# A decoder layer's attention projections: PSUM banks emptied by ScalarE copies, one ring of buffers, attention's loads queued later, last branch in another order

## The chip, the cores and the metric

The kernel runs on one core of one Trainium2 chip. A core has TensorE (PE: matmuls from SBUF into eight PSUM banks), VectorE (DVE), ScalarE (ACT), GpSimd (POOL) and SyncE (SP, whose queue issues most of the DMA loads here); each engine works through its own list of instructions in order. The metric is the device time of one execution in microseconds, and the time of a kernel is the median of its runs.

## The reference

A layer with 1024 tokens, width 1024, in fp32. One projection of h = RMSNorm(x) gives all inputs of three branches: A (attention of each query over 256 keys, which a small indexer picks), B (latent attention) and M (attention over 256 memory tokens). Each branch has a SiLU gate path z and a sigmoid merge gate.

```python
proj = h @ w_in[layer]
q_a = partial_rope(rms_norm(q_a.reshape(b, s, A_HEADS, A_HEAD_DIM), g_qn_a[layer]), cos_a, sin_a)
k_a = partial_rope(rms_norm(k_a.reshape(b, s, A_HEADS, A_HEAD_DIM), g_kn_a[layer]), cos_a, sin_a)
o_a = dsa_attention(q_a, k_a, v_a, q_i, k_i, w_i)
...
ys = jnp.stack([o_a * jax.nn.silu(z_a), o_b * jax.nn.silu(z_b), o_m * jax.nn.silu(z_m)])
branch = jnp.einsum('nbsw,nwd->nbsd', ys, w_branch[layer])
merged = jnp.einsum('bsnd,nbsd->bsd', gates, branch)
x = x + merged @ w_out[layer]
```

RMSNorm of q and k is over the 64 elements of a head; the rotation (`partial_rope`) turns its first 16. It is linear, so a factor per token and head may be applied before it or behind it.

## The kernel before

Every fp32 product is made of three matmuls (`mm3`, L273 to L275): each operand is split into a rounded part h and a rest l, and h·h, h·l and l·h are added in PSUM. Weights are loaded by SP (L258), then ACT casts the part h (L241) and DVE subtracts it to get l (L244); an output of 512 columns over 512 channels takes 12 matmuls.

The order of the program after the latent branch and the indexer is: branch 2 (M), branch 1 (B), the last projections, attention A with the matmuls of gate 0 as filler (`f`), the last branch 0 (A), and the output projection. `branch(n)` makes the gate path z (L1269, L1270), multiplies it with the loaded attention output `osb` (L1300, L1302) and splits the result into `yh` and `yl` (L1305, L1306); this is done for four pieces w of 128 channels, each in two halves j. Then `br` matmuls go over eight output blocks d, two halves j each; the merge gate `tg` (L1318) is loaded, and `emit` multiplies it with the bank (L1340 for `ab`, L1346 for `am`) and stores into `s_acc` by a DMA that POOL issues. In branch 0 (L1551 to L1563) `ac` is loaded back, POOL adds, ACT casts `hTh` and DVE subtracts to `hTl`, which feed the output projection. Before, branch 0 takes first the pieces whose z isn't made yet (w=3), then 0, 1, 2.

`qkv(p)` (p from 0 to 3) projects q, k and v of two heads of branch A: eight token tiles of 128 tokens, each 24 matmuls of 384 columns into one PSUM bank, in two halves of four tiles. qkv(0) stands in branch 2 between the y pieces and the `br` matmuls, qkv(1) in branch 1 likewise, then come z of branch 0 for w=0 (`early(0, 1)`), qkv(2), z for w=1, qkv(3), z for w=2. Four instructions of DVE and two of ACT read a tile's bank; the last is the subtraction of the rest of v:

```python
nc.scalar.activation(sq.rearrange("p h d -> p (h d)"), ps[:, 0:256], AF.Square)
nc.vector.tensor_reduce(out=ss[:, i, :], in_=sq, op=ALU.add, axis=AX.X)
for e, dst in enumerate((xq, xk)):
    nc.vector.tensor_tensor(dst[:, i], psv[:, e], g_am[:, e:e + 1, :].to_broadcast([P, 2, 64]), op=ALU.mult)
nc.scalar.copy(vst[:, i, 0::3, :], pv)
i_ = nc.vector.tensor_tensor(vst[:, i, 1:3, :], pv, f(vst[:, i, 0::3, :]), op=ALU.subtract)
run_topk(i_, 4.2)
```

`run_topk` lets the indexer's search for the 256th largest score run in the background. Its tests are `kdj` on DVE (L1039) and `kag` on ACT (L1045), which wait for the small updates `kac`, `kar`, `kaT` on DVE; an instruction of it stands behind the given one if both are on the same engine. Per half, POOL makes the reciprocal root `rr` (L234), scales q (L1389), DVE rotates (L422 to L427) and scales k (L1392), and ACT and DVE split q (L1393, L1394). `load_k` and `load_q` (L1407, L1413) load what attention A needs first (`akd`, `aqs`); the filler's weights are `f_0_0r` and so on (L389).

Of the kernel before, what the change touches and what calls it, by code (L numbers as in the profile page):

```python
# [16 lines left out]
ALU = mybir.AluOpType  # L17
# [78 lines left out]
def f(ap):  # L96
    return ap.bitcast(F32)
# [3 lines left out]
def hybrid_kernel(  # L101
# [144 lines left out]
    def wload(pool, nm, srcs, a, n, kind=None):  # L246


        def tile(dt, tag, bufs, nm, width):
            if width is None:  # L250
                return pool.tile([P, a, n], dt, tag=tag, name=nm, bufs=bufs)
            t = pool.tile([P, width], dt, tag=tag, name=nm, bufs=bufs)
            return t[:, 0:a * n].rearrange("p (a n) -> p a n", a=a)
        width = pool_raw[2] if len(pool_raw) > 2 else None
        raw = tile(F32, "raw", pool_raw[0], nm + "r", width)
        o = 0
        for ap, w in srcs:
            nc.sync.dma_start(raw[:, :, o:o + w], ap)  # L258
# [895 lines left out]
    wkind = [None]  # L1154
# [129 lines left out]
    def branch(n, zc, wpool, wk, yp, o_T, emit, bg=None, tgb=2, wkt=None, zb=2, ob=2, mid=None):  # L1284
# [3 lines left out]
        def b_weights(d):  # L1288
            return wload(wpool, f"b{n}w{d}", [(wview(w_branch[n], 0, 4, d * P, P), P)], 4, P, wkind[0])

        for w in sorted(range(4), key=lambda w: (n, w) in z_done):
            szs = z_part(n, w, zc, wpool, wk, zb)
            if n == 0 and b0 is None:
                b0 = b_weights(0)
            h_ = yp.tile([P, S], FR, tag=f"yh{w}", name=f"yh{n}_{w}")
            l_ = yp.tile([P, S], FR, tag=f"yl{w}", name=f"yl{n}_{w}")
            for j in range(2):
                cs = slice(j * 512, (j + 1) * 512)
                osb = wk.tile([P, 512], F32, tag="osb", name=f"osb{n}_{w}_{j}", bufs=ob)
                nc.sync.dma_start(osb, o_T[w * P:(w + 1) * P, cs])  # L1300
                sz = szs(j)
                i_ = nc.vector.tensor_tensor(sz, osb, sz, op=ALU.mult)  # L1302
                if bg is not None:
                    bg(i_, 5.1)
                nc.scalar.copy(h_[:, cs], sz)  # L1305
                nc.vector.tensor_tensor(l_[:, cs], sz, f(h_[:, cs]), op=ALU.subtract)  # L1306
            yh[w], yl[w] = h_, l_
        if mid is not None:
            mid()
        for d in range(NK):  # L1310
# [3 lines left out]
            for j in range(2):  # L1314
                cs = slice(j * 512, (j + 1) * 512)
                tg = (wkt or wk).tile([P, 512], F32, tag="tg", name=f"tg{n}_{d}_{j}", bufs=tgb)
# [12 lines left out]
    with w3s as ph:  # L1329
# [20 lines left out]
        def qkv(p):  # L1350
# [7 lines left out]
            ws[:] = WSG  # L1358
            for j in range(2):
# [4 lines left out]
                ss = wk.tile([P, 4, 4], F32, tag="ass", name=nm + "ss")  # L1364
                rr = wk.tile([P, 4, 4], F32, tag="arr", name=nm + "rr")
                vst = wk.tile([P, 4, 4, 64], FR, tag="vst", name=nm + "v", bufs=1)
                qs = wk.tile([P, 4, 2, 2, 64], FR, tag="qs", name=nm + "qs", bufs=1)
                for i in range(4):
# [6 lines left out]
                    psv = ps[:, 0:256].rearrange("p (e h d) -> p e h d", e=2, h=2)  # L1375
                    sq = wk.tile([P, 4, 64], F32, tag="asq", name=f"asq{p}_{tb}", bufs=1)
                    nc.scalar.activation(sq.rearrange("p h d -> p (h d)"), ps[:, 0:256], AF.Square)
                    nc.vector.tensor_reduce(out=ss[:, i, :], in_=sq, op=ALU.add, axis=AX.X)
                    for e, dst in enumerate((xq, xk)):
                        nc.vector.tensor_tensor(dst[:, i], psv[:, e], g_am[:, e:e + 1, :].to_broadcast([P, 2, 64]),  # L1380
                                                op=ALU.mult)
# [15 lines left out]
                nc.gpsimd.dma_start(s_qa[p][j], f(qs).rearrange("p t h e d -> p (t h e d)"))  # L1397

# [23 lines left out]
        branch(2, C_ZM, wpool, wk, yp, s_om, emit_b, run_topk, tgb=3, ob=2, mid=lambda: qkv(0))  # L1422
        branch(1, C_ZB, wpool, wk, yp, s_o[1], emit_m, run_topk, tgb=3, ob=2, mid=lambda: qkv(1))
# [13 lines left out]
    wkind[0] = None  # L1437


    with ExitStack() as ph:  # L1440
# [88 lines left out]
        attention(load_gen, k_prep, q_prep, scores, pv, pool_filler(fp, take_jobs("F", NFA), FWA, FBB), PFA, PREA, GENA, LDA)  # L1529
# [5 lines left out]
    with ExitStack() as ph:  # L1535
# [7 lines left out]
        with ExitStack() as ph2:  # L1543
# [5 lines left out]
            def emit_a(d, j, tg, pb):  # L1549
# [6 lines left out]
                late.append((d, j, ac))  # L1556

# [11 lines left out]
            pre = []  # L1569

            def pre_wo(after, pe):
                pre.append(0)
                if len(pre) == PRW:
                    pool_raw[:] = [1, 8]
                    wo_load(wpa, 0)
                    pool_raw[:] = list(PRF)
# [49 lines left out]
```

## Time and profile before

| | us |
|---|---|
| median of three runs | 1425.96 (1423.29 to 1428.38) |
| profiled execution | 1430.6, its span 1428.8 |
| PE busy | 1370.9 (96%) |
| PE's weight loads | 1173.3 |
| DVE busy | 954.4 (67%) |
| ACT busy | 681.4 (48%) |
| POOL busy | 209.3 (15%) |
| granted clock of TensorE, mean | 0.987 of 2.4 GHz |

The profiled execution is the one whose trace is read below; it took 4.6 us more than the median. Times in the trace count from the span's start. The stretch of the change runs from about 710 (qkv(0)) to 1060 (attention A begins), and the last branch from about 1264 to 1330.

### The profile page before, as it was taken

Reading aid. Unit: us, or ns where it says so; the run is one execution under the profiler, and the core shown is the slowest. Engines: PE = TensorE matmul, PEld = TensorE weight load, DVE = VectorE, ACT = ScalarE, POOL = GpSimd, SP = SyncE. Lnnn points to the kernel's source line nnn. Section 1 sums busy time; section 2 is a strip of 40 time slices with the busy share of each in tenths; the row PEclk is TensorE's granted clock in tenths of the full one; section 3 lists DMA queues with packets and bytes.
Section 4 is the critical chain, followed back from the end, with each engine's and each line's share of the span. In section 5 each row is a group of like instructions: output and inputs, shape, how many; then the busy total and the mean of one; then the engine's idle time right before and its main releaser. Section 6 shows DMA issues by size and latency. Waiting matters only on the chain.

```text
span 1428.8 us, 20870 instructions
## 1 busy us (share of the span) xinstructions
PE 1370.9 (96%) x7440; PEld 1173.3 (82%) x7440; DVE 954.4 (67%) x2434; ACT 681.4 (48%) x1464; POOL 209.3 (15%) x240
## 2 busy tenths in 40 slices
PE   7999999999999999999999999997999999988998
PEld 5998888888888889877897898796978888866787
DVE  5935446678888851578868777667868888756411
ACT  6635533356666652455655564433245666543200
POOL 3150004511102000000013004204220000004200
PEclk9999999999999999999999999998999999999999
DMA  7411222321111131012416532973151442175532
GB/s 246 135 45 54 77 58 86 114 56 41 49 56 53 45 104 46 23 52 67 132 52 231 164 85 89 255 165 118 46 180 49 126 133 59 54 234 186 185 105 71
DMA packets 154712, 147.45 MB, mean 103 GB/s; under 512 B 38000, under 2 KB 114800, under 8 KB 154608
## 3 DMA queue, kind: packets, MB, share of 16 engines
q1 hardware_dynamic: 147024, 123.58, 29.0%
q0 software_dynamic: 7008, 20.45, 4.8%
q10 hardware_dynamic: 576, 2.10, 0.4%
q8 instruction: 58, 0.95, 0.3%
q14 instruction: 46, 0.38, 0.1%
HBM read 99.43 MB, written 46.66 MB: 102 GB/s over the span
## 4 chain that ended last, share of the span: by engine, by line
PE 64%; DVE 13%; ACT 6%; issue 6%; DMA 5%; POOL 3%; SPq 0%; ACTq 0%; DVEq 0%; POOLq 0%
PE f L273 6%; PE f L274 5%; PE f L275 5%; DVE kdj L1039 2%; PE o L274 2%; PE o L273 2%; PE o L275 2%; PE br L275 2%; PE br L273 2%; ACT kag L1045 2%; PE br L274 2%; DVE idx L1233 1%; PE ixps L274 1%; PE ixps L275 1%; PE ixps L273 1%
## 5 line engine op out<-in xcount | busy, mean ns | idle before, releaser
L1045 ACT ACTIVATE kag<-idx,kaT 128x896 bf16<-128x896 f32 (+2 forms) x96 | 82.8, 862 | 42.2 <-DVE kaT L1066 37.9
L1039 DVE TENSOR_SCALAR_CACHE_REDUCE kdj<-idx,kdT 128x1024 bf16<-128x1024 f32 (+2 forms) x96 | 92.3, 962 | 0.7
L273 PE MATMUL f<-hTh,f_0h 128*128 128x512 f32 x184 | 79.4, 432 | 4.9 <-DVE sz L1270 2.8
L273 PE MATMUL f<-hTh,f_1h 128*128 128x512 f32 x184 | 76.3, 415 | 0.0
L274 PE MATMUL f<-hTl,f_0h 128*128 128x512 f32 x184 | 75.0, 408 | 0.0
L275 PE MATMUL f<-hTh,f_0l 128*128 128x512 f32 x184 | 74.9, 407 | 0.0
L275 PE MATMUL f<-hTh,f_1l 128*128 128x512 f32 x184 | 74.3, 404 | 0.0
L274 PE MATMUL f<-hTl,f_1h 128*128 128x512 f32 x184 | 73.9, 401 | 0.0
L1554 POOL TENSOR_TENSOR ac<-ac,tg 128x512 f32<-128x512 f32 x16 | 25.0, 1565 | 265.2 <-DVE tg L1552 257.3
L1596 DVE TENSOR_TENSOR xr<-o,xr 128x512 f32<-128x512 f32 x16 | 11.0, 690 | 61.8 <-PE o L275 61.8
L365 ACT ACTIVATE fo<-f 128x512 f32<-128x512 f32 x48 | 28.8, 600 | 39.9 <-PE f L275 36.0
L1227 ACT ACTIVATE irl<-is 128x512 f32<-128x512 f32 (+1 forms) x80 | 37.8, 527 | 15.6 <-DVE idx L1233 12.0
L273 PEld LDWEIGHTS f<-hTh,f_0h 128*128 128x128 f32 x184 | 35.5, 193 | 11.6 <-ACT fo L365 3.1
L1233 DVE SCALAR_TENSOR_TENSOR idx<-irl,wi,idx 128x1024 f32<-128x1024 f32 (+5 forms) x42 | 40.2, 958 | 2.5 <-ACT irl L1227 0.8
L275 PEld LDWEIGHTS f<-hTh,f_0l 128*128 128x128 f32 x184 | 35.7, 194 | 6.8
L275 PEld LDWEIGHTS f<-hTh,f_1l 128*128 128x128 f32 x184 | 34.7, 189 | 6.0
L274 PEld LDWEIGHTS f<-hTl,f_0h 128*128 128x128 f32 x184 | 35.7, 194 | 3.9
L274 PEld LDWEIGHTS f<-hTl,f_1h 128*128 128x128 f32 x184 | 34.9, 190 | 4.4
L273 PEld LDWEIGHTS f<-hTh,f_1h 128*128 128x128 f32 x184 | 35.0, 190 | 4.2
L1225 PE MATMUL is<-kih,iqT 128*128 128x512 f32 (+1 forms) x80 | 30.1, 381 | 2.7 <-ACT irl L1227 2.3
L1270 DVE SCALAR_TENSOR_TENSOR sz<-sz,z 128x512 f32<-128x512 f32 x24 | 16.3, 683 | 23.4 <-ACT sz L1269 23.4
L1174 DVE TENSOR_SCALAR wi<-ixps 128x8 f32<-128x8 f32 x8 | 1.3, 166 | 42.0 <-ACT xi L1172 42.0
(1237 smaller groups left out, 4765.4 us busy)
## 6 DMA issues: line engine op xcount, KB each, us to landing
s_tg<-fo SPq DMA_DIRECT2D x48, 256.0 KB, 2.1
tg<-s_tg SPq DMA_DIRECT2D x48, 256.0 KB, 4.7
f_0r<-in_w_in_dram SPq DMA_DIRECT2D x23, 256.0 KB, 3.2
f_1r<-in_w_in_dram SPq DMA_DIRECT2D x23, 256.0 KB, 3.2
xx<-in_x_dram SPq DMA_DIRECT2D x8, 512.0 KB, 7.2
osb<-s_o SPq DMA_DIRECT2D x16, 256.0 KB, 3.0
s_acc<-ab POOLq DMA_DIRECT2D x16, 256.0 KB, 5.1
s_acc<-am POOLq DMA_DIRECT2D x16, 256.0 KB, 6.2
```

The source lines that it names most:

```text
L273: nc.tensor.matmul(ps, ah, bh, start=start, stop=False)
L274: nc.tensor.matmul(ps, ah, bl, start=False, stop=False)
L275: nc.tensor.matmul(ps, al, bh, start=False, stop=stop)
L365: nc.scalar.activation(o, ps, AF.Tanh, scale=0.5)
L1039: nc.vector.tensor_scalar(out=junk, in0=idx[t], scalar1=T[:, i:i + 1], scalar2=0.0, op0=ALU.is_ge, op1=ALU.add, accum_out=cnt[:, i:i + 1])
L1045: nc.scalar.activation(junk, idx[t], AF.Sign, bias=T[:, i:i + 1], accum_out=cnt[:, i:i + 1])
L1225: nc.tensor.matmul(sp[:, 0:w], q_, kih[:, k0:k0 + w], start=True, stop=False)
L1227: nc.scalar.activation(rl[:, k0:k0 + m], sp[:, 0:m], AF.Relu)
L1233: i_ = nc.vector.scalar_tensor_tensor(out=acc[:, 0:n], in0=rl[:, 0:n], scalar=wc, in1=acc[:, 0:n], op0=ALU.mult, op1=ALU.add)
L1270: zi[0] = nc.vector.scalar_tensor_tensor(out=sz, in0=sz, scalar=1.0, in1=pz[j], op0=ALU.add, op1=ALU.mult)
L1554: nc.gpsimd.tensor_tensor(ac, ac, tg, op=ALU.add)
L1596: nc.vector.tensor_tensor(xr, ps, xr, op=ALU.add)
```

## The change

- In `qkv`, ACT copies q, k and v of a token tile out of the bank (three copies of 128x128), and nothing else reads the bank. Squares, sums, the gain and the split of v are then made once per half, over 512 columns.
- q and k are rotated before they are scaled by `rr`; POOL scales both (before, q on POOL and k on DVE).
- `run_topk` is given the copy of v, an ACT instruction.
- `tg`, `ab`, `am`, the copies of q, k, v and the squares share a ring of nine buffers (`t2k`); before, `tg` had three, `ab` and `am` three, the others their own.
- `load_k(0)`, `load_q(0, ·)` and the filler's first weights are put behind the last weight load of qkv(3) in SP's queue.
- Branch 0 makes z of w=3 first and then the y pieces in the order 0, 1, 2, 3; its weights `b0w` have a ring of their own, with two raw buffers instead of one; the output weights `wo` are started at the fourth output instead of the eighth y piece.

```diff
-PRF = (1, 5)
+WOD = (1, 1)
+PRF = (2, 2)
...
-        for w in sorted(range(4), key=lambda w: (n, w) in z_done):
-            szs = z_part(n, w, zc, wpool, wk, zb)
-            if n == 0 and b0 is None:
-                b0 = b_weights(0)
+        early_z = {}
+        if n == 0:
+            for w in range(4):
+                if (n, w) not in z_done:
+                    early_z[w] = z_part(n, w, zc, wpool, wk, zb)
+            b0 = b_weights(0)
+        for w in range(4):
+            szs = early_z.pop(w, None) or z_part(n, w, zc, wpool, wk, zb)
...
+        def t2k(nm):
+            return wk.tile([P, 512], F32, tag="t2k", name=nm, bufs=9)
...
         def emit_b(d, j, tg, pb):
-            ac = wk.tile([P, 512], F32, tag="ac", name=f"ab{d}_{j}", bufs=3)
+            ac = t2k(f"ab{d}_{j}")
...
-                xq = wk.tile([P, 4, 2, 64], F32, tag="xq", name=nm + "xq")
-                xk = wk.tile([P, 4, 2, 64], F32, tag="xk", name=nm + "xk", bufs=1)
+                sh = "p (t h d) -> p t h d"
+                xq, xk, xv = (t2k(f"{nm}x{c}").rearrange(sh, t=4, h=2) for c in "qkv")
...
+                    psv = ps.rearrange("p (e h d) -> p e h d", e=3, h=2)
+                    for e, x_ in enumerate((xq, xk, xv)):
+                        i_ = nc.scalar.copy(x_[:, i], psv[:, e])
                     run_topk(i_, 4.2)
+                for e, x_ in enumerate((xk, xq)):
+                    sq = t2k(f"{nm}sq{e}").rearrange("p (t d) -> p t d", t=8)
+                    nc.scalar.activation(sq, x_.rearrange("p t h d -> p (t h) d"), AF.Square)
+                    nc.vector.tensor_reduce(out=ss[:, e, :], in_=sq, op=ALU.add, axis=AX.X)
+                    nc.vector.tensor_tensor(x_.rearrange("p t h d -> p (t h) d"), x_.rearrange("p t h d -> p (t h) d"),
+                                            g_am[:, 1 - e:2 - e, :].to_broadcast([P, 8, 64]), op=ALU.mult)
                 rsqrt_mean(rr, ss, 1.0 / 64)
...
+                for e, x_ in enumerate((xk, xq)):
+                    rope(x_[:, :, :, 0:16], cos_a[:, b, :], sin_a[:, b, :], 2, 8, wk, f"ar{p}_{j}_{e}")
+                    r_ = rr[:, e, :].rearrange("p (t h) -> p t h", t=4).unsqueeze(3).to_broadcast([P, 4, 2, 64])
+                    nc.gpsimd.tensor_tensor(x_, x_, r_, op=ALU.mult)
+                nc.scalar.copy(vst[:, :, 0::3, :], xv)
+                nc.vector.tensor_tensor(vst[:, :, 1:3, :], xv, f(vst[:, :, 0::3, :]), op=ALU.subtract)
...
-        load_k(0)
-        load_q(0, 0)
-        load_q(0, 1)
         early(1, 2)
-        qkv(3)
+        a3 = qkv(3)
+        with tc.issue_after(a3.ins):
+            load_k(0)
+            load_q(0, 0)
+            load_q(0, 1)
...
+                if (d, j) == WOD:
+                    pool_raw[:] = [1, 8]
+                    wo_load(wpa, 0)
+                    pool_raw[:] = list(PRF)
```

ACT's list at the start of qkv(2), where `z0w` are the next gate path's weights, `f_0_0h` the filler's, `asq` and `a_0v` the readers of the banks `a_0` to `a_2`; before:

```order
L241 CAST z0w_0h<-z0w_0r 128x512
L241 CAST z0w_4h<-z0w_4r 128x512
L1377 ACTIVATE asq_0_10253<-a_0_10228 128x256
L241 CAST f_0_0h<-f_0_0r 128x512
L1383 CAST a_0v<-a_0_10228 128x2x64
L1377 ACTIVATE asq_1_10289<-a_1_10264 128x256
L1383 CAST a_0v<-a_1_10264 128x2x64
L241 CAST f_0_1h<-f_0_1r 128x512
L1377 ACTIVATE asq_2_10325<-a_2_10300 128x256
L1383 CAST a_0v<-a_2_10300 128x2x64
L241 CAST f_1_0h<-f_1_0r 128x512
```

and now:

```order
L241 CAST z0w_4h<-z0w_4r 128x512
L1270 ACTIVATE sz_0_1_10156<-z_0_1_10125 128x512
L1386 COPY a_0xq<-a_0_10209 128x128
L1386 COPY a_0xk<-a_0_10209 128x128
L1386 COPY a_0xv<-a_0_10209 128x128
L1386 COPY a_0xq<-a_1_10241 128x128
L1386 COPY a_0xk<-a_1_10241 128x128
L1386 COPY a_0xv<-a_1_10241 128x128
L1386 COPY a_0xq<-a_2_10273 128x128
```

The three casts of filler weights no longer stand between the readers of the banks (they are now in qkv(3)).

SP's queue at the same place, where `akd` and `aqs` are attention's first loads, `z0w` the weights of z for w=1, and `a3w0r` to `a3w3r` those of qkv(3); before:

```order
L258 DMA a2w3r<-in_w_in_dram 128x2x128 x3
L1407 DMA akd_10617<-s_ka_0_112 128x8x64
L1407 DMA akd_10617<-s_ka_1_113 128x8x64 x2
...
L1413 DMA aqs_1_10625<-s_qa_1_105 128x4x128
L258 DMA z0w_0r<-in_w_in_dram 128x4x128
L258 DMA z0w_4r<-in_w_in_dram 128x4x128
L389 DMA f_0_0r<-in_w_in_dram 128x4x128
L258 DMA a3w0r<-in_w_in_dram 128x2x128 x3
L258 DMA a3w1r<-in_w_in_dram 128x2x128 x3
L389 DMA f_0_1r<-in_w_in_dram 128x4x128
L389 DMA f_1_0r<-in_w_in_dram 128x4x128
```

and now:

```order
L258 DMA a2w3r<-in_w_in_dram 128x2x128 x2
L258 DMA z0w_0r<-in_w_in_dram 128x4x128
L258 DMA z0w_4r<-in_w_in_dram 128x4x128
L258 DMA a3w0r<-in_w_in_dram 128x2x128 x3
L258 DMA a3w1r<-in_w_in_dram 128x2x128 x3
L258 DMA a3w2r<-in_w_in_dram 128x2x128 x3
L258 DMA a3w3r<-in_w_in_dram 128x2x128 x3
L1418 DMA akd_11050<-s_ka_0_112 128x8x64 x2
...
L1424 DMA aqs_1_11058<-s_qa_1_105 128x4x128
L258 DMA z0w_0r<-in_w_in_dram 128x4x128
L258 DMA z0w_4r<-in_w_in_dram 128x4x128
L390 DMA f_0_0r<-in_w_in_dram 128x4x128
```

All weights of qkv(3) now stand ahead of attention's loads and of the filler's.

SP's queue at the start of the last branch, where `osb` and `sz` (the stored z of w=0 to 2) feed the y pieces, and `b0w2r` and `wo_0r` are weights; before:

```order
L366 DMA s_tg_99<-fo_7_1_13918 128x512
L1300 DMA osb_3_0_14007<-s_o_95 128x512
...
L1300 DMA osb_0_1_14032<-s_o_95 128x512
L258 DMA wo_0r<-in_w_out_dram 128x2x512
L1318 DMA tg_1_0_14142<-s_tg_99 128x512
L1551 DMA ac_0_14157<-s_acc 128x512
L1300 DMA osb_1_0_14041<-s_o_95 128x512
L1318 DMA tg_1_1_14163<-s_tg_99 128x512
L1254 DMA sz_0_0_14027<-s_z 128x512
...
L1300 DMA osb_1_1_14048<-s_o_95 128x512
L258 DMA wo_1r<-in_w_out_dram 128x2x512
...
L258 DMA b0w2r<-in_w_branch_dram 128x4x128
```

and now:

```order
L258 DMA b0w2r<-in_w_branch_dram 128x4x128
L258 DMA b0w3r<-in_w_branch_dram 128x4x128
...
L367 DMA s_tg_99<-fo_7_1_13878 128x512
...
L1305 DMA osb_0_0_13967<-s_o_95 128x512
L1255 DMA sz_0_0_13969<-s_z 128x512
L1305 DMA osb_0_1_13974<-s_o_95 128x512
L1255 DMA sz_0_1_13976<-s_z 128x512
L1305 DMA osb_1_0_13983<-s_o_95 128x512
L1255 DMA sz_1_0_13985<-s_z 128x512
...
L1305 DMA osb_3_1_14023<-s_o_95 128x512
...
L258 DMA wo_0r<-in_w_out_dram 128x2x512
L258 DMA b0w4r<-in_w_branch_dram 128x4x128
```

`sz_0_0` follows right behind `osb_0_0`, `b0w2r` and `b0w3r` are ahead of every load of a y piece, and `wo_0r` is behind them all.

## Rows read from the trace of the kernel before

**Rows 1.** The page, busy time: us (share of the span) xinstructions.

```profile
PE 1370.9 (96%) x7440; PEld 1173.3 (82%) x7440; DVE 954.4 (67%) x2434; ACT 681.4 (48%) x1464; POOL 209.3 (15%) x240
```

**Rows 2.** What PE waited for, 740 to 1060 us: total, times, longest.

```profile
PE a L273 <- DVE a_0v L1384: 7.0, 2, 5.8
PE a L274 <- DVE a3w3l L244: 3.8, 1, 3.8
PE br L273 <- DVE a_1v L1384: 3.3, 2, 2.4
PE f L273 <- DVE sz L1270: 2.8, 1, 2.8
PE br L273 <- DVE ab L1340: 2.3, 2, 1.4
```

**Rows 3.** The same view, 1260 to 1335 us.

```profile
PE br L275 <- DVE b0w2l L244: 4.4, 1, 4.4
PE br L273 <- ACT yh L1305: 3.9, 1, 3.9
```

**Rows 4.** Sum over the six windows at half clock: us, busy of each engine.

```profile
sum 34.50, PE 28.00 PEld 23.05 DVE 23.44 ACT 10.42 POOL 15.07; mean PE 4.67 PEld 3.84 DVE 3.91 ACT 1.74 POOL 2.51
```

**Rows 5.** One window in branch 2: us, busy (x), clock, DMA share, GB/s.

```profile
775.00:800.00 25.00, 25.00 (x108) 20.10 (x107) 19.13 (x51) 14.79 (x30) 5.39 (x10) 1.00 0.84 276
```

**Rows 6.** What ACT waited for, 935 to 975 us.

```profile
ACT z0w_0h L241 <- DMA z0w_0r<-in_w_in_dram: 5.0, 1, 5.0
...
ACT f_0h L241 <- DMA f_0r<-in_w_in_dram: 3.1, 1, 3.1
```

**Rows 7.** Timeline of SP's queue, 936 to 988 us: start, us, instruction.

```profile
936.58 4.38 SPq L1413 DMA_DIRECT2D aqs<-s_qa  x4
941.06 0.61 SPq L258 DMA_DIRECT2D z0w_0r<-in_w_in_dram  x1
...
985.24 1.39 SPq L258 DMA_DIRECT2D a3w3r<-in_w_in_dram  x3
```

**Rows 8.** ACT's groups by form, 710 to 1045 us: busy, mean ns, idle before.

```profile
L1045 ACT ACTIVATE kag<-idx,kaT 128x896 bf16<-128x896 f32 x27 | 28.1, 1043 | 38.3 <-DVE kaT L1066 36.3 <-DVE kdT L1066 2.0
...
L1377 ACT ACTIVATE asq<-a 128x256 f32<-128x256 f32 x32 | 12.1, 377 | 0.0
...
L1383 ACT CAST a_0v<-a 128x128 fp32r<-128x128 f32 x16 | 4.2, 261 | 29.3 <-DVE a_0xk L1380 29.3
L1393 ACT CAST a_0qs<-a_0xq 128x512 fp32r<-128x512 f32 x4 | 2.5, 621 | 17.7 <-DVE a_0xq L427 11.3 <-issue 6.4
```

**Rows 9.** DVE's groups by form, the same stretch.

```profile
L1392 DVE TENSOR_TENSOR a_0xk<-a_0xk,a_0rr 128x512 f32<-128x512 f32 x4 | 2.7, 683 | 0.0
```

**Rows 10.** Timeline of POOL, 1034 to 1041 us.

```profile
1035.10 2.92 POOL L234 TENSOR_TENSOR a_1rr<-a_1rr,mhalf 128x16 f32<-128x16 f32 x1
...
1038.39 1.05 POOL L1389 TENSOR_TENSOR a_1xq<-a_1xq,a_1rr 128x512 f32<-128x512 f32 x1
```

**Rows 11.** Tile `am`: its store by DMA, us to landing.

```profile
DMA to landing us min/median/max: 4.8/6.2/7.5
```

**Rows 12.** Tile `tg`, 740 to 930 us: its load, us to landing.

```profile
DMA to landing us min/median/max: 2.6/5.6/8.8
```

**Rows 13.** Timeline of SP's queue, 1264 to 1282 us.

```profile
1265.19 1.89 SPq L1300 DMA_DIRECT2D osb<-s_o  x4
...
1273.55 1.38 SPq L1254 DMA_DIRECT2D sz<-s_z  x3
...
1281.90 0.43 SPq L258 DMA_DIRECT2D b0w2r<-in_w_branch_dram  x1
```

**Rows 14.** Tile `osb`, 1264 to 1290 us: its load, us to landing.

```profile
DMA to landing us min/median/max: 2.8/4.7/5.8
```

**Rows 15.** Timeline, POOL and DVE, 1292.9 to 1296 us.

```profile
1293.74 1.10 DVE L1563 SCALAR_TENSOR_TENSOR hTl<-ac,hTh 128x512 fp32r<-128x512 f32 x1 [1.25 <-ACT hTh L1555]
```

**Rows 16.** Timeline of DVE, 1041 to 1044 us.

```profile
1042.31 1.28 DVE L1270 SCALAR_TENSOR_TENSOR sz<-sz,z 128x512 f32<-128x512 f32 x2
```

More of the change, by code (lines that the diff above doesn't have):

```diff
@@ L1315, in branch @@
                 cs = slice(j * 512, (j + 1) * 512)
[L1316 removed]
+                tg = (wkt or wk).tile([P, 512], F32, tag=tgt, name=f"tg{n}_{d}_{j}", bufs=tgb)
                 if (n, d) in gates_done:
@@ L1344, in emit_m @@
         def emit_m(d, j, tg, pb):
-            ac = wk.tile([P, 512], F32, tag="ac", name=f"am{d}_{j}", bufs=3)
+            ac = t2k(f"am{d}_{j}")
             i_ = nc.vector.scalar_tensor_tensor(out=ac, in0=tg, scalar=1.0, in1=pb, op0=ALU.add, op1=ALU.mult)
@@ L1358, in qkv @@
             ws[:] = WSG
+            last = last_load[0]
             for j in range(2):
@@ L1374, in qkv @@
                         mm3(ps, ah, al, wh[:, kt % 2, :], wl[:, kt % 2, :], kt == 0, kt == NK - 1)
[L1375 to L1381, printed above, removed]
@@ L1386, in qkv @@
                 rsqrt_mean(rr, ss, 1.0 / 64)
-                nc.gpsimd.tensor_scalar(out=rr[:, :, 0:2], in0=rr[:, :, 0:2], scalar1=64 ** -0.5,
+                nc.gpsimd.tensor_scalar(out=rr[:, 1, :], in0=rr[:, 1, :], scalar1=64 ** -0.5,
                                         scalar2=0.0, op0=ALU.mult, op1=ALU.add)
-                nc.gpsimd.tensor_tensor(xq, xq, rr[:, :, 0:2].unsqueeze(3).to_broadcast([P, 4, 2, 64]), op=ALU.mult)
-                for e, v in enumerate((xk, xq)):
-                    rope(v[:, :, :, 0:16], cos_a[:, b, :], sin_a[:, b, :], 2, 8, wk, f"ar{p}_{j}_{e}")
@@ L1397, in qkv @@
                 nc.gpsimd.dma_start(s_qa[p][j], f(qs).rearrange("p t h e d -> p (t h e d)"))
+            return last
         hds = ExitStack()
@@ L1420, in early @@
                 z_early(0, w, C_ZA, wpool, wk, run_topk)
-        branch(2, C_ZM, wpool, wk, yp, s_om, emit_b, run_topk, tgb=3, ob=2, mid=lambda: qkv(0))
-        branch(1, C_ZB, wpool, wk, yp, s_o[1], emit_m, run_topk, tgb=3, ob=2, mid=lambda: qkv(1))
+        branch(2, C_ZM, wpool, wk, yp, s_om, emit_b, run_topk, ob=2, mid=lambda: qkv(0))
+        branch(1, C_ZB, wpool, wk, yp, s_o[1], emit_m, run_topk, ob=2, mid=lambda: qkv(1))
         early(0, 1)
@@ L1528, in hybrid_kernel @@
         ws[:] = WSQ
-        attention(load_gen, k_prep, q_prep, scores, pv, pool_filler(fp, take_jobs("F", NFA), FWA, FBB), PFA, PREA, GENA, LDA)
+        fill_a = pool_filler(fp, take_jobs("F", NFA), FWA, FBB)
+        with tc.issue_after(a3.ins):
+            fill_a.run(1)
+        attention(load_gen, k_prep, q_prep, scores, pv, fill_a, PFA, PREA, GENA, LDA)
     hds.close()
@@ L1568, in hybrid_kernel @@
             pool_raw[:] = PRF
[L1569 to L1576, printed above, removed]
+            wkind[1] = ("wb", 6, 512)
             ws[:] = WSF
-            branch(0, C_ZA, wpool, wkz, yp, s_o[0], emit_a, pre_wo, 4, wk, ZB5, OB5)
+            branch(0, C_ZA, wpool, wkz, yp, s_o[0], emit_a, None, 4, wk, ZB5, OB5, tgt="tg")
             ws[:] = WSO
```

22 lines of the change are left out of this document (9 added, 13 removed).

## The prediction

> **What bounds the kernel now.** The page's first part comes first: PE is busy for 1370.9 of 1428.8 us [rows 1], so what can be won without fewer matmuls is its idle time, and time in which it works at the lower clock. Next I read what PE waited for, over the two stretches that the change touches. Between 740 and 1060 us PE waits 7.0 us for `a_0v` and 3.3 for `a_1v`, which are DVE's last reads of a projection's bank; 3.8 for the low part of qkv(3)'s last weights; 2.8 for `sz`, which holds the filler's bank; and 2.3 for `ab` [rows 2]. In the last branch it waits 4.4 us for `b0w2l` and 3.9 for the first `yh` [rows 3]. Together that is 27.5 us.
>
> Third, I looked for windows in which the granted clock is half (0.51, the level of 1.2 GHz). There are six after 800 us, at 882, 967, 994, 1042, 1278 and 1298, and each lies at one of the waits of 2.4 us or more; behind waits of 1.4 us or less there was none. In these 34.5 us PE is busy for 28.0 [rows 4], work that takes 14.0 at the full clock (2.4 GHz): they cost 14.0 us, 2.3 each on average. The ceiling for this change is so 27.5 + 14.0 = 41.5 us. The step of a matmul of 512 columns at full clock is 25.00 us / 108 = 0.23 [rows 5], an output of the branches (12 of them) 2.8.
>
> Why are the banks late? Around the longest wait (it ends at 970) ACT had stood for 5.0 us before the weights `z0w_0r` and 3.1 before `f_0r` [rows 6], and SP issued `z0w_0r` only at 941.06, behind 4.38 us of `aqs` issues [rows 7]. ACT's casts of v also stood 29.3 us for DVE's `a_0xk` [rows 8]. So ACT and DVE pass each other's delays on, and the bank comes free when both are through. In the last branch the loads of `sz` start at 1273.55, 8.4 us after the first `osb` at 1265.19, and `b0w2r` at 1281.90 [rows 13].
>
> **The change, part by part.**
>
> *Banks.* ACT's three copies per tile take at most 0.26 us each by the cast of the same shape, 0.8 against 0.38 + 0.26 before; per half ACT gets two squares and the cast of v, about 0.62 each by the cast of 512 columns [rows 8]. That is 4 × 0.14 + 3 × 0.62 = 2.4 us more per half of some 17, on an engine that is busy for 48% [rows 1]. No copy waits for DVE now, and the casts of filler weights have left this place. What is late next is ACT itself behind `kag` tests (1.04 us the longest, and 38.3 us of idle time before them [rows 8]). Bound: 10.3 us gained if ACT is always in time, nothing if the tests hold it as DVE did. Banks are reused two to four tiles later, so I take 9.3.
>
> *Weights of qkv(3).* Their last load was issued at 985.24 [rows 7]; now it is ahead of attention's and the filler's loads. Gain 3.8, bound 0 to 3.8. Attention's loads cost nothing: they have qkv(3) as cover, 192 matmuls of three quarters of 0.23, or 33 us; without it each 4.7 us (the landing of `osb`, the same 256 KB [rows 14]) would show.
>
> *The filler's bank.* `sz` was read at 1042.31 [rows 16], behind the split of q, which waited for POOL's root and product, 2.92 and 1.05 us [rows 10]. Now its first half stands ahead of that split, behind reductions, gains and rotations that need no root. The squares, sums, gains, 12 rotations and the split of v add up to about 7 us after the last tile, so some 1.5 us of the wait stays: gain 1.3, bound -1 to 2.8.
>
> *`ab`.* The wait of 1.4 came from DVE behind POOL, and goes; the other 0.9 followed a late weight, and stays. Gain 1.4.
>
> *Last branch.* `sz_0_0` follows the first `osb`, so it lands near 1265.7 + 4.7 = 1270.4 [rows 13, 14], and the first `yh` comes 1.3 us later, ahead of the end of z (about 1275.6: before, `sz` landed near 1278.2, `yh` came at 1279.5, and PE had waited for 3.9). DVE's chain of 18 operations of 0.68 [rows 9] ends near 1282.8; PE needs the last piece after some 30 matmuls, at 1282.5. `b0w2` is loaded before the branch. `b0w3l` stands behind the product of `tg_2_0` on DVE, at about 1290.9, and PE needs it at 1292.3. Both waits go, 8.3 us, but two places are just in time: gain 7.3, bound 4 to 8.3.
>
> *Clock.* If no wait of 2.4 us or more stays, all 14.0 come back; if two stay, 9.4.
>
> *The ring.* `tg` was loaded ahead of the projections; now a load waits for a buffer five outputs back. One pass is a store (6.2 [rows 11]), a load (5.6 [rows 12]) and a DVE operation (0.68): 12.5 us, and PE gives 5 × 2.8 = 13.9. With the longest landings it is 7.5 + 8.8 + 0.7 = 17.0, 3.1 too long; three passes in a branch make 9.3, less the 5.6 that PE may run ahead over its banks, plus a half clock of 2.3: 6 per branch, 12 for two. The typical landing gives nothing; as the first loads come late too, I take 4. What is queued behind such a load on SP are the next weights of the same branch.
>
> The Trainium skill, DMA: Bandwidth & Descriptors, section "Anatomy of one DMA — SWDGE (gpsimd) path", gives a DMA as about 2.0 us plus its bytes over 436 GB/s. An estimate from it for 256 KB is 2.6, so that a pass would be 5.9 us, the ring would never wait, and the sum would be 37 instead of 33. The trace doesn't agree: its median store takes 6.2 us [rows 11].
>
> *Sum.* 9.3 + 3.8 + 1.3 + 1.4 + 7.3 + 14.0 - 4 = 33 us. The profiled execution took 1430.6, so it would take about 1397.5; the median of the runs is 4.6 below it, 1425.96, and becomes 1393.
>
> **The rivals.**
>
> *The ring binds.* Landings near the long end of both rows, because copies, stores and loads now run together (the DMA share is 0.84 there already [rows 5]). The gain of 37 loses 12, and up to 7 more if weights behind a waiting load are late too: 18 to 25 us gained, 1401 to 1408. For it speaks the load of 8.8; against it the medians.
>
> *ACT is the new keeper of the banks.* If `kag` tests, each waiting for DVE's update, hold the copies for longer than the spare banks last, the 9.3 and the half clocks at three waits (7) don't come: 33 - 16 = 17 gained, 1409. For it speak 38.3 us of idle time before `kag`; against it, that qkv(2) and qkv(3), where the longest waits are, have few tests.
>
> *POOL slows DVE.* DVE's `hTl` took 1.10 us beside a POOL addition [rows 15], where operations of that shape take 0.68 [rows 9]. POOL gets eight more products of 1.05 us [rows 10]. If one meets the chain ahead of `sz`, the wait of 1.5 grows by 0.4 to 1.05, to about 2.4, and the half clock comes back: 1 + 2.3 less, 30 gained, 1396. The Trainium skill, GPSIMD Engine Reference, section "Key points", says that POOL shares its SBUF interfaces with VectorE and collides with its instructions of two SBUF inputs; by that rule this is the case, and the row agrees.
>
> *Slower than before.* One mechanism can do it: the ring's pass grows until it sets the pace of both branches. Each branch loses 3 × (L - 13.9) - 5.6. For the 37 us to be lost in two branches, L has to be 21.9 us; the longest store and the longest load together give 17.0. A store that waits behind POOL's other work, and a load behind a weight on SP, could add some us; 22 in every pass is hard to see.
>
> **How the numbers follow.** Chances: the sum as worked out, with or without POOL's part, 0.62 (own range 1385 to 1401); the ring 0.16; ACT 0.12; slower 0.05; no measurable change 0.03, if several of these meet; better than 1385, 0.02. The predicted time is 1393. The range takes in the bounds of the ring and of ACT: 1383 to 1411. About 0.3% (4 us) is what a measurement of this kernel can tell from no change: faster by more 0.92, within it 0.03, slower 0.05.
>
> **What would show it.** In the changed profile PE's waits for `a` and `br` on a DVE read of the bank are gone and those on ACT's copies are short; a3w3l is gone from the list; the windows at half clock in the last branch are gone; `b0w3l` and `yl` wait under 1 us. The prediction is wrong if PE waits in `br` for `ab` or `am` several times per branch, each after a `tg` load that waited for an `s_acc` store, if `z` or `a` waits for weights queued behind them, or if attention's first transposes wait for `akd`.

## The result, and the profile after

| | us, median (range, runs) | ratio to the kernel before, 95% interval |
|---|---|---|
| before | 1426.15 (1423.29 to 1428.38, 4) | |
| changed | 1437.66 (1436.91 to 1442.87, 4) | 1.009 [1.006, 1.0119] |

The change makes the kernel 0.9% slower, where 2.3% faster was forecast. The profiled execution took 1442.87 us, 5.2 above the median; its span is 1441.1.

The page's busy times, as in [rows 1]:

```profile
PE 1366.4 (95%) x7440; PEld 1169.4 (81%) x7440; DVE 956.4 (66%) x2338; ACT 692.7 (48%) x1520; POOL 222.8 (15%) x248
```

PE's busy time fell by 4.5 us, but its idle time grew from 57.9 to 74.7. What PE waited for between 740 and 1075 us (total, times, longest), which answers to [rows 2]:

```profile
PE br L274 <- DVE am L1354: 12.4, 5, 4.7
PE br L274 <- DVE ab L1348: 8.5, 4, 4.0
PE z L274 <- ACT kag L1046: 4.3, 1, 4.3
PE z L276 <- DVE z1w_4l L244: 2.9, 3, 1.3
PE z L274 <- ACT a_1xv L1386: 1.4, 1, 1.4
PE f L274 <- DVE sz L1271: 1.2, 1, 1.2
PE a L274 <- ACT a_0xv L1386: 1.0, 1, 1.0
```

The waits at which the change was aimed are gone or short: `a_0v` and `a_1v` have become 2.4 us on ACT's copies (before 10.3), `a3w3l` is no longer there, `sz` fell from 2.8 to 1.2. In their place stand 20.9 us for `am` and `ab`, the products with `tg`, of which 2.3 were there before. The row of `kag` most likely belongs to them: its wait ends at 948.36, just behind the branch's last `am` (947.52 to 948.21), and before, the same matmul of z waited 0.6 us for `am`; by the profile `kag` only ended a little later. The same view in the last branch, 1268 to 1350 us, answers to [rows 3]:

```profile
PE br L274 <- ACT b0w6h L241: 8.6, 1, 8.6
PE br L276 <- DVE b0w6l L244: 1.6, 1, 1.6
PE br L274 <- ACT yh L1310: 1.2, 1, 1.2
PE br L276 <- DVE b0w3l L244: 0.6, 1, 0.6
```

Here too the old waits went (`yh` and `b0w2l`, 8.3 us in all, are down to 1.8 with `b0w3l`), and a later weight is waited for 10.2 us.

The stretches at half clock are now others as well: five, two in branch 1 and one in each of branch 2, the z path behind branch 1 and the last branch, each at one of the new waits. Their sum (us, busy of each engine) answers to [rows 4]:

```profile
sum 36.50, PE 23.25 PEld 17.99 DVE 25.69 ACT 15.53 POOL 13.76; mean PE 4.65 PEld 3.60 DVE 5.14 ACT 3.11 POOL 2.75
```

The windows are wider than the stretches (their mean clock is 0.50 to 0.72), so half of the 23.25, 11.6 us, is the most that they cost, against 14.0 before.

Comparing the starts of the same matmuls in the two traces: from the first matmul of qkv(2) to that of qkv(3), with z between them, it takes 44.98 us (before 54.84), from there to attention A's first transposition 50.03 (52.07), the stretch from attention A's first transposition to the last branch's first matmul 230.55 (240.03), and from there to the first matmul with `b0w3` 18.74 (27.39). That is 30.0 us gained. But branch 2 (first matmul with `b2w0` to z of branch 1) takes 55.86 (48.85), the z path behind it 3.6 more, and branch 1 with its z path 80.66 (61.14): 30 us lost. The last branch loses another 12.7 between `b0w3` and the output projection. The rest of this document is about these two losses.

**Where SP stands in branch 2.** SP's queue before and in the changed kernel, around the sixth, seventh and eighth weights of branch 2 (start, us, instruction):

```profile
758.85 1.85 SPq L1318 DMA_DIRECT2D tg<-s_tg  x2
761.69 0.38 SPq L258 DMA_DIRECT2D b2w5r<-in_w_branch_dram  x1
762.33 0.47 SPq L1318 DMA_DIRECT2D tg<-s_tg  x1
765.25 0.38 SPq L258 DMA_DIRECT2D b2w6r<-in_w_branch_dram  x1
765.85 2.20 SPq L1318 DMA_DIRECT2D tg<-s_tg  x2
772.25 0.38 SPq L258 DMA_DIRECT2D b2w7r<-in_w_branch_dram  x1
```

```profile
758.52 0.38 SPq L258 DMA_DIRECT2D b2w5r<-in_w_branch_dram  x1
759.01 0.51 SPq L1323 DMA_DIRECT2D tg<-s_tg  x1
760.84 0.38 SPq L258 DMA_DIRECT2D b2w6r<-in_w_branch_dram  x1
761.27 2.24 SPq L1323 DMA_DIRECT2D tg<-s_tg  x2
770.58 0.38 SPq L258 DMA_DIRECT2D b2w7r<-in_w_branch_dram  x1
771.07 1.39 SPq L1323 DMA_DIRECT2D tg<-s_tg  x3
```

Counted from the branch's first, 5, 6 and 8 loads of `tg` stood ahead of `b2w5r`, `b2w6r` and `b2w7r` before; now it is 2, 3 and 5. Every weight load is followed at once by `tg` loads: it is the weight that waits, and the `tg` loads stand behind it. What SP waited for, 756 to 800 us:

```profile
SPq L258 <- DVE b2w3l L244: 14.1, 1, 14.1
...
SPq L258 <- DVE b2w5l L244: 7.0, 1, 7.0
...
```

The first row is where it starts: SP stands for 14.1 us at `b2w5r`, until DVE has split `b2w3l` behind the work on qkv(0), and the third load of `tg` stands behind that weight. `b2w7r` needs the raw buffer of `b2w5r`, which is free when DVE has split it. And DVE, 758 to 771 us:

```profile
764.88 0.69 DVE L1348 SCALAR_TENSOR_TENSOR ab<-tg,br 128x512 f32<-128x512 f32 x1 [4.11 <-DMA tg<-s_tg]
...
768.33 0.69 DVE L1348 SCALAR_TENSOR_TENSOR ab<-tg,br 128x512 f32<-128x512 f32 x1 [0.42 <-DMA tg<-s_tg]
...
769.86 0.69 DVE L244 TENSOR_TENSOR b2w5l<-b2w5r,b2w5h 128x512 fp32r<-128x512 f32 x1
```

The split of `b2w5l` stands behind two `ab`, and the first of these had waited 4.1 us for its `tg`. So the loop is closed: a `tg` is late, DVE stands at the `ab` that needs it, the split behind that `ab` is late, SP stands at the weight that needs the split's buffer, and the next three `tg` behind that weight are late. The stores play no part here: POOL issued those of the first three `ab` at 758.46, 759.39 and 765.87, and with the typical landing of 3.6 us (first row below) the last of them was through at about 769.5, ahead of `b2w7r`. Landings are no longer than before. The tiles `ab`, `am` and `tg`, 740 to 950 us, which answer to [rows 11, 12]:

```profile
DMA to landing us min/median/max: 2.3/3.6/6.1
DMA to landing us min/median/max: 3.8/5.3/7.7
DMA to landing us min/median/max: 2.7/5.2/7.2
```

**Where SP stands in the last branch**, 1304 to 1333 us:

```profile
1304.85 0.38 SPq L258 DMA_DIRECT2D wo_1r<-in_w_out_dram  x1
...
1314.88 0.38 SPq L258 DMA_DIRECT2D wo_2r<-in_w_out_dram  x1
...
1324.39 0.38 SPq L258 DMA_DIRECT2D wo_3r<-in_w_out_dram  x1
...
1326.09 0.42 SPq L258 DMA_DIRECT2D b0w6r<-in_w_branch_dram  x1
```

The `wo` loads follow one another by 13.5 (the first is at 1291.32), 10.0 and 9.5 us, and `b0w6r` stands behind the last of them. They have one raw buffer, but SP does not wait for it here: the splits of `wo_0`, `wo_1` and `wo_2` had ended 3.3, 1.6 and 1.6 us before the next `wo` load went out. What SP and POOL waited for, 1290 to 1336 us:

```profile
SPq L1323 <- POOL ac L1569: 24.5, 9, 7.5
...
POOL ac L1569 <- DMA ac<-s_acc: 14.0, 3, 6.5
```

SP stands at `tg` loads whose buffers POOL's addition frees, and POOL stands for `ac` loads that come behind these in SP's queue: a loop like that of branch 2. It lets `b0w6r` out 38.7 us behind the branch's first matmul, nearly as before (39.4). PE, though, now asks for this weight after 36.4 us (before it came to it after 44.2), so the gain at the branch's start is lost at this wait. Before, the first `wo` load was issued at 1267, ahead of half of the y pieces, and the last at 1293.5, ahead of `b0w3` to `b0w7`.

### The profile page after: what moved, and what is told of

The parts are those of the page before. It is cut to its first block, busy times and chain, and to the rows that moved or that the text cites. A ratio compares the mean times of both kernels' runs of the same rounds, so it can differ in the third digit from the quotient of the medians.

```text
span 1441.1 us, 20833 instructions
## 1 busy us (share of the span) xinstructions
PE 1366.4 (95%) x7440; PEld 1169.4 (81%) x7440; DVE 956.4 (66%) x2338; ACT 692.7 (48%) x1520; POOL 222.8 (15%) x248
## 3 DMA queue, kind: packets, MB, share of 16 engines
q1 hardware_dynamic: 147024, 123.58, 28.9%
## 4 chain that ended last, share of the span: by engine, by line
PE 61%; DVE 15%; ACT 7%; DMA 7%; issue 6%; POOL 2%; SPq 1%; DVEq 0%; POOLq 0%; ACTq 0%
PE f L274 6%; PE f L275 5%; PE f L276 5%; DVE kdj L1040 3%; PE o L275 2%; PE o L276 2%; PE o L274 2%; DMA tg<-s_tg 2%; ACT kag L1046 2%; DVE idx L1234 1%; PE ixps L275 1%; PE ixps L276 1%; PE ixps L274 1%; PE b_3pt L463 1%; PE qmps L276 1%
## 5 line engine op out<-in xcount | busy, mean ns | idle before, releaser
L233 POOL TENSOR_SCALAR a_0rr<-a_0ss 128x16 f32<-128x16 f32 x4 | 3.7, 930 | 171.2 <-DVE a_0ss L1391 171.2
```

## Experiments

Two theories of branches 2 and 1: **Store** (the ring: a `tg` load waits for a store to land, as the prediction's ring term has it) and **Queue** (the loop above: the place of the `tg` loads among the weights in SP's order). For the last branch: the **chain** of `wo` loads through their one raw buffer. The kernel before ran beside each group of four; its medians are 1426.15 us in the first (own buffers, eight, eight with three, the old trigger), 1424.01 in the second (order alone, (7, 1), (4, 1), fourth half) and 1424.93 in the third (parts alone, (6, 1)). Ratios are to these.

### `tg` with buffers of its own

```diff
-def branch(..., tgb=9, ..., tgt="t2k"):
+def branch(..., tgb=3, ..., tgt="tg"):
...
-            return wk.tile([P, 512], F32, tag="t2k", name=nm, bufs=9)
+            return wk.tile([P, 512], F32, tag="t2k", name=nm, bufs=6)
```

Expected: 

> The changed kernel, but the loads of tg have three buffers of their own again (as before the change), and ab, am and the x tiles share six. Two theories of why branches 2 and 1 lost about 30 us. Queue: SP works in order, the loads of tg now stand behind weight loads that wait for a split on DVE, and DVE stands at an ab or am that waits for a tg. Store: a ring of nine is too short for one pass of store, load and product. Both say that the loss goes: 1438 - 28 = about 1410 us (1405 to 1415), and PE's waits for am and ab shrink from 21 us to under 4. If the loss is neither (ACT's or POOL's new work), the time stays at 1434 to 1440.

Measured: 1407.52 us, 0.9875 [0.9857, 0.9893]. The loss of both branches goes: PE's waits for `am` and `ab`, 740 to 1075 us, are 3.7 us in all. Both theories said so; what it shows is that the loss hangs on the shared ring and not on ACT's or POOL's new work, which is all still there.

### A ring of eight; and with it three raw buffers

```diff
-def branch(..., tgb=9, ..., tgt="t2k"):
+def branch(..., tgb=8, ..., tgt="t2k"):
...
-            return wk.tile([P, 512], F32, tag="t2k", name=nm, bufs=9)
+            return wk.tile([P, 512], F32, tag="t2k", name=nm, bufs=8)
```

Expected: 

> The changed kernel with a ring of eight buffers in place of nine; the order of the loads on SP stays as it is. Store: a pass has half an output (1.4 us) to a whole one (2.8 us) less room, at three to four passes in a branch that is 4 to 11 us per branch more: 1446 to 1458 us. Queue: what a load waits for is mostly the weight ahead of it, so a buffer more or less costs little: 1435 to 1443 us.

Measured: 1438.44 us, 1.0093 [1.0071, 1.0114], as the changed kernel. A buffer less costs nothing: the ring's length doesn't bind, which speaks against Store.

With the same ring of eight, the raw buffers:

```diff
-                    pool_raw[:] = [2, 8, 768]
+                    pool_raw[:] = [3, 8, 768]
```

Expected: 

> The changed kernel with a ring of eight, and three raw buffers for weights in place of two, so that a weight load waits for the split of the third weight before it, not of the second. Queue: the weights no longer hold up the loads of tg behind them, most of the loss in branches 2 and 1 comes back: 1412 to 1428 us. Store: the weights change nothing and the ring is shorter: 1446 to 1458 us.

Measured: 1435.76 us, 1.0073 [1.0056, 1.0089]: neither number came. SP's queue and its waits in this run, 756 to 777 us:

```profile
757.18 0.38 SPq L258 DMA_DIRECT2D b2w7r<-in_w_branch_dram  x1
757.62 2.14 SPq L1323 DMA_DIRECT2D tg<-s_tg  x2
767.07 0.38 SPq L258 DMA_DIRECT2D z1w_0r<-in_w_in_dram  x1
767.50 1.46 SPq L1323 DMA_DIRECT2D tg<-s_tg  x3
```

```profile
SPq L258 <- DVE b2w5l L244: 7.2, 1, 7.2
...
```

SP stands just as long for the same split `b2w5l`, only that the weight that stands there is the next one, `z1w_0r`: with a buffer more, every weight moved one place forward in the queue, past the `tg` loads, and `z1w_0r` has the same five of them ahead of it as `b2w7r` had. My form of Queue was wrong in that it blamed the weights' buffers; what counts is how many `tg` loads stand ahead of the weight at which SP stops.

### The ring as it is, the order alone changed

```diff
+for n_ in (2, 1):
+    HOLD.update({f"b{n_}w5": (n_, 2, 1), f"b{n_}w6": (n_, 3, 0), f"b{n_}w7": (n_, 3, 1),
+                 f"z{n_ - 1}w0_0": (n_, 4, 1), f"z{n_ - 1}w0_4": (n_, 5, 1)})
+HOLD.update({"z1w1_0": (2, 6, 1), "z1w1_4": (2, 7, 1), "a2w0": (1, 6, 1)})
...
-            last_load[0] = nc.sync.dma_start(raw[:, :, o:o + w], ap)
+            with tc.issue_after(tg_load[HOLD[nm]].ins) if nm in HOLD else ExitStack():
+                last_load[0] = nc.sync.dma_start(raw[:, :, o:o + w], ap)
```

Here `tg_load` keeps the load of each `tg`, and a weight in `HOLD` is issued behind the one that is named. Lines of this kernel are up to seven higher.

Expected: 

> The changed kernel with the shared ring of nine as it is; only the order on SP is another: weights 5 to 7 of branches 2 and 1 and the first weights of what follows are held back behind loads of tg, so that from tg_2_1 on SP's order is that of the run in which tg had buffers of its own. Queue (place of the tg loads among the weights): most of the loss of branches 2 and 1 comes back, 1408 to 1418 us. Ring (it is the sharing of the buffers, by whatever release, that makes tg late, and weights held back behind it are late too): 1435 to 1445 us. The last branch is untouched and keeps its loss.

Measured: 1408.75 us, 0.9885 [0.9867, 0.9902]. Nine shared buffers, the same stores, and 28.9 us less than the changed kernel (26.8 if each is set against the kernel before beside it). SP's queue, 757 to 783 us:

```profile
759.05 1.51 SPq L1330 DMA_DIRECT2D tg<-s_tg  x2
760.61 2.31 SPq L264 DMA_DIRECT2D b2w5r<-in_w_branch_dram  x1
763.02 0.66 SPq L1330 DMA_DIRECT2D tg<-s_tg  x1
763.77 0.44 SPq L264 DMA_DIRECT2D b2w6r<-in_w_branch_dram  x1
764.31 0.64 SPq L1330 DMA_DIRECT2D tg<-s_tg  x1
770.53 0.38 SPq L264 DMA_DIRECT2D b2w7r<-in_w_branch_dram  x1
```

`b2w7r` is issued when it was in the changed kernel (770.53 against 770.58), but here all `tg` up to `tg_3_1` are ahead of it, where there `tg_2_0` was the last: 6, 7 and 8 loads of `tg` stand ahead of the three weights, as in the run with buffers of its own. The tiles `ab` and `am` show that Store fails in its premise too, for these stores land later than in the changed kernel, and PE has no wait for `ab` or `am` that follows a `tg` load held by a store. (SP waited for one once, 3.1 us at 909.8; PE's one long wait in branch 1, 3.4 us for `am`, comes from DVE's work ahead of it.)

```profile
DMA to landing us min/median/max: 2.5/5.3/7.0
DMA to landing us min/median/max: 4.5/6.4/8.2
```

### The last branch: when `wo` is asked for

First the old trigger (the eighth half of y) in the changed kernel.

```diff
-                if (d, j) == WOD:
-                    wo_load(wpa, 0)
...
+            def pre_wo(after, pe):
+                pre.append(0)
+                if len(pre) == 8:
+                    wo_load(wpa, 0)
```

Expected: 

> The changed kernel, but the loads of wo are asked for at the eighth half of y again, as before the change, not at output (1, 1). My theory of the last branch: b0w6r stands behind wo_3r on SP, and the four wo loads follow one another through one raw buffer about 9.7 us apart, so b0w6 comes late (PE waits 8.6 us, and a half clock of 10 us behind it). Then the wait for b0w6h goes and the time falls by 8 to 13 us: 1425 to 1430 us. Rival: b0w6r waits for the low part of an earlier b0 weight on DVE; then nothing changes (1436 to 1440), or the early wo loads hold up the weights of the branch's start, and it is slower.

Measured: 1436.37 us, 1.007 [1.0055, 1.0085]; 1.3 us less, which the intervals don't tell from nothing. `b0w6h` is in time, but PE waits for the weight ahead of it (1260 to 1345 us):

```profile
PE br L274 <- ACT b0w5h L241: 4.8, 1, 4.8
PE br L276 <- DVE b0w3l L244: 2.6, 1, 2.6
```

The y pieces now come first in SP's queue, so even by the old trigger `wo_0r` is issued 14.1 us behind the first matmul of the last z (before 3.2) and `wo_3r` 42.3 us behind it (before 29.6), with `b0w5r` behind that. The size that I expected was wrong, because I took the old trigger for the old place.

The other four runs stand on the kernel with buffers for `tg` alone (1407.52 us) and differ in the trigger only (`WOD = (7, 1)`, `(4, 1)`, `(6, 1)`, and `len(pre) == 4` in the edit above).

Expected at (7, 1): 

> The kernel with buffers for tg alone (1407.5 us), and wo asked for at output (7, 1): on SP b0w6r and b0w7r now stand ahead of wo_2r and wo_3r. Theory of the last branch: what waits is the b0 weight that stands behind a wo load, and the wo loads come one by one through their one raw buffer, some 9.7 us apart. Then the wait for b0w6h (9.2 us) and the half clock behind it go: 1394 to 1398 us. Rival: the wo weights then come too late for the output projection, which waits 8 us or more: 1403 to 1412 us.

Expected at (4, 1): 

> The kernel with buffers for tg alone (1407.5 us), and wo asked for at output (4, 1): on SP b0w4r, b0w5r and b0w6r each change places with the wo load ahead of them, nothing else moves. Theory of the last branch: b0w6r now waits for wo_2r's raw buffer alone, one step of the chain (about 9.7 us) less: the wait of 9.2 us for b0w6h falls to 1 us or less, 1394 to 1399 us. Rival: b0w6r waits for its own raw buffer (the split of b0w4) or DVE; then the wait stays over 6 us and the time over 1403.

Expected at the fourth half of y: 

> The kernel with buffers for tg alone (1407.5 us), and wo asked for at the fourth half of y: the chain of the wo loads starts earlier, but b0w5r and b0w6r stand behind all four. By the theory of the chain wo_3r is issued some three steps of 9 to 10 us after wo_0r, at about the third output's time, and b0w5 is then late by 2 to 5 us: 1399 to 1405 us. If instead the y halves are held up by osb loads behind wo_1r, the wait for yh or yl grows above 2 us.

Expected at (6, 1): 

> The kernel with buffers for tg alone, with wo asked for at output (6, 1): on SP b0w6r stands ahead of wo_2r, as at (7, 1), and b0w7r behind it. At (7, 1) the output projection began 6.5 us late, because of waits of 2.5 us for hTh and 1.1 for hTl among the splits of wo_3, at (4, 1) b0w6h was waited for 5.3 us. If the two ends trade off, this one has neither: 1394 to 1398 us. If b0w7 is late behind wo_2r, it has a wait of 2 to 5 us for b0w7h: 1399 to 1403 us.

| `wo` asked for at | us | ratio | PE's main waits in the branch and behind it |
|---|---|---|---|
| (1, 1) | 1407.52 | 0.9875 [0.9857, 0.9893] | `b0w6h` 9.2, `b0w6l` 1.6 |
| (4, 1) | 1400.23 | 0.9825 [0.9801, 0.9848] | `b0w6h` 5.3 |
| (7, 1) | 1399.66 | 0.9825 [0.9806, 0.9844] | `hTh` 2.5, `hTl` 1.1 in the output projection |
| fourth half of y | 1400.30 | 0.9825 [0.9808, 0.9842] | `b0w4h` 3.7, `b0w3l` 1.9 |
| (6, 1) | 1396.67 | 0.9808 [0.979, 0.9826] | `b0w7h` 1.4, `b0w7l` 1.4, `hTh` 1.3, `hTl` 0.7 |

The place of `wo` moves the `b0` weights in SP's queue: `b0w6r` stands behind 12 loads of `tg` and 11 of `ac` at (1, 1), 12 and 10 at (4, 1), 10 and 8 at (6, 1) and (7, 1). One place in the queue at (4, 1) took away 3.9 us of the wait, not the 8 or more that I had expected. At (7, 1) the `b0` weights are in time, but DVE stands for 3.1 us at the split of `wo_3` with products for `hT` behind it. (6, 1) trades the two ends off, and has the lowest median of the study; its interval overlaps those of the three runs above it.

The chain alone doesn't explain these times. With the fourth half of y it is there: SP waits 2.5, 2.6 and 0.7 us for the split of the `wo` load before, and `b0w4r` and `b0w5r` stand behind. At (1, 1) SP waits for POOL's additions instead, as above. That the trigger's place is worth 8 to 11 us is shown; how much of it is the raw buffer and how much the loop over POOL is not.

### Parts alone

The last branch's part on the kernel before (its early loads, its buffers, `wo` at (1, 1)), and the same with `wo` at (7, 1):

```diff
-PRF = (1, 5)
+PRF = (2, 2)
+WOD = (1, 1)
...
+            wkind[1] = ("wb", 6, 512)
```

Expected: 

> The kernel before, with the last branch's part of the change alone (early loads of sz, b0 weights in buffers of their own, wo at output (1, 1)). In the run with buffers for tg alone this part gained 8.4 us from the branch's start to its fourth weight and lost 14.5 from there to the end, and before the branch it also takes away the wait of 3.9 us for yh with some 2 us of half clock. If the parts add up: 1424 - 4 - 2 - 8.4 + 14.5 = about 1424 us (1421 to 1428), no gain. If its late weights were a consequence of the other parts, the loss of 14.5 isn't there: 1408 to 1413 us.

Measured: 1424.03 us, 0.9991 [0.9981, 1.0002]: no change, as the sum of the parts gave. PE waits 8.4 us for `b0w6h` here as well, so that wait belongs to this part alone.

Expected: 

> As the run before it in this list, but wo is asked for at output (7, 1), with b0w6r and b0w7r ahead of wo_2r on SP. By the theory of the wo chain it gains what that step gained with the rest of the change, 8 us: 1413 to 1419 us. If the parts hang together, no gain over it.

Measured: 1418.05 us, 0.9956 [0.994, 0.9971]: within the range, and 6.0 us less than with `wo` at (1, 1), where 8 were expected. The trigger's place gains without the other parts too.

Attention's loads and the filler's put back to their old place in SP's queue, with `tg`'s own buffers and `wo` at (7, 1):

```diff
-        a3 = qkv(3)
-        with tc.issue_after(a3.ins):
-            load_k(0)
-            load_q(0, 0)
-            load_q(0, 1)
+        qkv(3)
```

(the three calls stand ahead of `early(1, 2)` again, and the filler's first step has no `issue_after`.)

Expected: 

> The kernel with buffers for tg alone and wo asked for at (7, 1) (1399.7 us), with one part of the change undone: attention's first loads and the filler's stand on SP where they stood before, ahead of the last weights of qkv(3). If they are what made those weights late, PE waits for a3w3l again, 3.8 us and a half clock of 2.3 behind it: 1404 to 1408 us. Rival: the weights came late only because the banks did, and with the banks emptied by ACT the order of these loads is worth nothing: 1398 to 1402 us.

Measured: 1408.50 us, 0.9887 [0.9864, 0.991], 8.8 more than with them later. What PE waited for, 900 to 1060 us:

```profile
PE f L274 <- ACT fo L366: 3.2, 1, 3.2
PE a L274 <- ACT a3w2h L241: 2.1, 1, 2.1
PE a L275 <- DVE a3w2l L244: 1.4, 1, 1.4
```

The late weights are back (`a3w2` in place of `a3w3`), with a wait of the filler that I had not foreseen; each has a half clock behind it. This part of the change is worth more than the 3.8 us and one half clock that were forecast.

## Why the prediction was wrong

**The ring term is the step that failed.** It took 4 us for the ring; undoing the order alone, with the ring as it is, gives back 28.9. The error was not in the landings or in the 13.9 us of room: the typical landings were as assumed or shorter, and the run with later landings was the fast one. It was in the sentence "What is queued behind such a load on SP are the next weights of the same branch". That looks at what waits behind the load. What the load waits behind was the question: before, the `tg` loads stood ahead of the weights, with buffers that came free by DVE's own product; in the shared ring they could not be asked for so early (the first ones waited for DVE's last reads of the copies of q, k and v), and the weights, whose buffers are their own, moved past them. Then the wait of a weight for a split on DVE became part of the pass, and DVE's wait for `tg` part of the split. The argument read SP's new order for qkv(3) and for the last branch, and not for the loads of branches 2 and 1. Of the signs that it set for being wrong, the waits for `ab` and `am` came, nine of them, but not their second half: no `tg` load in front of them had waited for a store.

The rival on the slower side had the number nearly right for a reason that was only half named. By its formula, the 17.2 us that branch 1 lost (67.15 against 49.90 up to its successor's z) make a pass of 21.5 us, and the 7.0 of branch 2 one of 18.1; it asked for 21.9 in both. "A load behind a weight on SP, could add some us" was its last clause, and that was the mechanism, priced at a few us without looking at what the weight itself waits for. With that, its chance of 0.05 was far too low.

**The last branch was mis-sized on its far side.** The forecast gain at its start came: `yh` and `b0w2l` fell from 8.3 to 1.8 us with `b0w3l`, and "at about 1290.9, and PE needs it at 1292.3" was as tight as said (`b0w3l` 0.6). But the sum counted this gain of 7.3 as won, and had no term for what comes next: PE reaches `b0w6` 7.8 us sooner, and its load, with `wo` now put among the branch's weights, goes out when it always did. That cost 10.2 us of waits with a half clock; moving `wo` to (6, 1) gave back 10.9 (1407.52 to 1396.67).

**What held.**

- Banks: 9.3 forecast; of 10.3 us of waits 2.4 are left in the changed kernel (7.9 gained) and 1.1 with the order repaired (9.2). ACT was not the new keeper of the banks.
- Weights of qkv(3): 3.8 forecast, gone; undone, the whole part costs 8.8.
- The filler's bank: 1.3 forecast, 1.6 measured (2.8 to 1.2). The rival that POOL slows DVE there would have left 2.4. POOL's new products did slow DVE elsewhere: the split `b2w3l` took 3.02 us beside two of them (0.68 before), and just as long with the order repaired, where it cost nothing.
- `ab`: 1.4 forecast, not seen: 8.5 in the changed kernel, and with the order repaired 1.4 with 3.4 for `am`.
- Clock: 14.0 forecast if no wait of 2.4 us stayed. The new waits had 10.9 to 11.6 of their own; in the fastest run PE is busy for 1354.2 us, 16.7 less than before with as many matmuls.

So the sum's positive terms, taken together, came near. The 37 us without the ring would have been 1389 on the median of before. The run with buffers for `tg` alone and `wo` at (6, 1), which takes both losses away, took 1396.67; the order repaired and `wo` at (6, 1) together were not run. The 8 left are about the short waits that the sum did not have: `am` 2.0, `b0w7` 2.8, `hT` 2.0 and `a2w3l` 1.1.

The estimate from the Trainium skill, DMA: Bandwidth & Descriptors, "Anatomy of one DMA — SWDGE (gpsimd) path", 2.6 us for such a store, would have left the ring out of the sum. The trace still does not agree with it (medians of 3.6 to 6.4 us). The ring did not bind all the same: with the order repaired a typical pass, 6.4 + 5.6 + 0.7 = 12.7 us, is shorter than five outputs, 13.9.

## What to carry to other kernels

When a load's buffers are merged with others, read the new order of its queue first, and ask of each load which instruction ahead of it can stop the queue and what that one waits for; here a cycle through two in-order engines cost 29 us. A pool with buffers of its own buys a place in the queue, not only room. When a stage is made to start sooner, ask which load its next step needs and whether that comes sooner too (here `b0w6` did not), and when an early transfer is moved, look for the consumers that now stand behind it in the queue.

## What the runs showed of the hardware

Landings were shorter in the slower kernel: 256 KB stores took 3.6 and 5.3 us (`ab`, `am`) in the changed kernel and 5.3 and 6.4 in the faster one with the order repaired, so here a short landing went with loads that were issued late, and was no sign of a good order. And the length of a wait alone doesn't tell whether the clock falls: a wait of 2.0 us for `am` was enough in the fastest run, one of 1.8 in the run with attention's loads at their old place, and in the changed kernel one of 1.9 that ended at 917.8, where waits of 2.2 and 2.1 us that ended at 927.4 and 941.0 had none behind them. Before, 2.4 was the least that had one, and the prediction took that for a bound. A window of the fastest run behind that wait (us, busy of each engine, clock, DMA share, GB/s):

```profile
900.00:902.00 2.00, 2.00 (x6) 1.52 (x6) 1.90 (x7) 1.30 (x4) 0.75 (x1) 0.50 0.97 256
```
